# A hybrid decoder layer: sums of the features begun by item count instead of by the norm's factor, and another order of the first loads

## The chip, the core and the metric

The kernel runs on one core of a Trainium2 chip. A core has TensorE (matmuls; PE in the profile, with PEld for its weight loads), VectorE (DVE), ScalarE (ACT), GpSimd (POOL) and SyncE (SP), and 16 DMA engines that serve the queues of SP, ACT and POOL. The metric is the device time of one execution in microseconds; three runs of the kernel before took 2243.14, 2243.8 and 2244.31 us, the median is 2243.8.

## What is computed

One decoder layer on x of 256 tokens by 2048 features: a SwiGLU feed-forward, a token mixer (sliding-window attention beside an RWKV-7 recurrence), cross-attention into a memory of 256 tokens, a second SwiGLU feed-forward and a last norm. Only the first feed-forward and the last norm are touched:

```python
def rms_norm(x, g):
    y = xf * lax.rsqrt(jnp.mean(xf * xf, axis=-1, keepdims=True) + NORM_EPS)
    return (y * g.astype(jnp.float32)).astype(x.dtype)

def swiglu(h, w_gate, w_up, w_down):
    return (jax.nn.silu(h @ w_gate) * (h @ w_up)) @ w_down

x = x + 0.5 * swiglu(rms_norm(x, ffn1_norm[l]), ffn1_w_gate[l], ffn1_w_up[l], ffn1_w_down[l])
...
return rms_norm(x, final_norm)
```

The hidden width is 5632, so a gate or up matrix is 2048 x 5632 and 46 MB in float32. Everything is float32 in the reference.

## The kernel before

**Products.** Each float32 factor is split into a high part (rounded to the fp32r format) and the remainder. A product is three matmuls (lines 434 to 436): high by high, high by low, low by high. Weights come in units of two slabs of 128 rows by 512 columns. ScalarE makes the high part `hi` (line 357), VectorE the remainder `lo` (line 358), in rings of three buffers. Each use of a unit is an *item*: `next_item` hands out item i, and divides up to two units beyond it. In a plain product, an item is 12 matmuls (two slabs, two halves of the tokens, three matmuls).

**Seven products for eight.** In most of the feed-forward, gate and up are computed together, and for some items ("seven": 0, 2 and 4 of the eight pairs in a block of the first feed-forward) eight block products are replaced by seven, as in Strassen's and Winograd's schemes. This needs sums of weight slabs (`divide`, lines 386 to 389, split by `two_parts` into `thi` and `tlo`, lines 365 and 366) and sums and differences of the features (`combinations`, lines 466 to 485: sums on VectorE, a cast `chi` on ScalarE, the remainder `clo` on VectorE). A seven item is 21 matmuls, one of the others 24. The features' sums are made once for a feed-forward and used by all its pair products.

**The first feed-forward.** The norm's gain is applied to the features as they arrive (`Norm.features`: `xhi` in lines 653 and 655, `xlo` in line 656), the factor 1/rms only behind the products, since it is one number for each token. So the first block of gate (items 0 to 7) and of up (items 8 to 15) run as plain products while the sum of squares is still being made from x in its other layout (`tokens`, `squares`, line 667). `rstd` turns it into the factor `rs` (two small operations on VectorE, one power on POOL, lines 681 to 684). From item 16 on come the pairs, which need the sums of the features.

**Order of work.** A planner of the framework places the instructions on the engines from the order in which the program writes them. Background steps are Python generators; `bg.tick()` advances each group by one step, twice in a plain item. `combinations` is one of them: it does nothing until `ready()` holds, then takes three ticks for each of five pairs of features (0 to 4). The first pair product does not go on before they are all written (`bg.until(lambda: c["done"] ...)`). `tc.issue_after(at["lo"].ins)` puts a step behind the newest `lo` on VectorE; `at["hi"]` does so on ScalarE. In the kernel before, `ready()` is: the factor is written, and item 5 has begun.

**The first loads.** `cols` holds the gains, 16 columns of 128 partitions. `chunks(c, n)` loads n feature chunks of 128 features by 256 tokens, transposed, on SP's queue. `load(u, pieces)` loads weight units: in this stage a buffer holds four slabs (units u and u+1), of which there are four. Before, ScalarE's queue takes `cols` and the first slab; SP's takes features 0-1, slab 1, slabs 2-3, features 2-3, slabs 4-5, slabs 6-7, features 4-7 and so on.

Of the kernel before, what the change touches and what calls it, by code (L numbers as in the profile page):

```python
# [7 lines left out]
F32 = mybir.dt.float32  # L8
# [19 lines left out]
KU = 2  # L28
# [108 lines left out]
def decoder_layer(ctx: ExitStack, tc: tile.TileContext, a: dict, out: bass.AP):  # L137
# [102 lines left out]

    cols = cpool.tile([P, 163], F32, name="cols")
    cpool.tile([P, P], F32, name="pad")
    act.dma_start(cols[:, :KD], a["cols"][:, :KD])
    g_ffn1, g_mix, g_cross, g_mem, g_ffn2 = (cols[:, i * KD : (i + 1) * KD] for i in range(5))
    w0, a0, k_k, k_a, r_k, ln_w, ln_b = (cols[:, 80 + i * 8 : 88 + i * 8] for i in range(7))
    mu = cols[:, 136:163]
# [48 lines left out]
    def load(u, pieces=None):  # L295

        if u >= len(units) or u in raws:
            return
        w, k, c0, n = units[u]
        wide = at["pool"] is not None and (u < ends[0] or u >= ends[1] + LOADED)  # L300
        m = 2 if wide else 1
        if wide:
            raw = at["pool"].tile([P, m * KU, n], F32, tag="raw2", name="raw2", bufs=4)
        else:
            raw = wp.tile([P, KU, n], F32, tag="raw", name="raw", bufs=4)
        for i in range(m):
            raws[u + i] = raw[:, i * KU : (i + 1) * KU, :]
        if u in first_unused:
            second = u + 1 in first_unused
            pieces = [(slice(1, 2), nc.sync)] + [(slice(2 + second, 4), nc.sync)]  # L310
            if not second:
                pieces = ((slice(1, 4), nc.sync),)
        elif u + 1 in first_unused and wide:
            pieces = ((slice(0, 2), nc.sync), (slice(3, 4), nc.sync))
        for i, queue in pieces or ((slice(0, m * KU), nc.sync),):
            rows = slice((k + i.start) * P, (k + i.stop) * P)
            queue.dma_start(raw[:, i], w[rows, c0 : c0 + n].rearrange("(a p) n -> p a n", p=P))

    def load_sums(i):

# [367 lines left out]
    def feed_forward(sp, x, norm: Norm, wg, wu, wd, done, begin_last=lambda: None, last=False):  # L688
        if last:
            for tag, shape, dt, bufs in (  # L690
                ("hhi", [P, 16, T], F32R, 1), ("hlo", [P, 16, T], F32R, 1),
                ("hb", [P, 2, 512], F32, 2), ("thia", [P, KU, 512], F32R, 1),
                ("tloa", [P, KU, 512], F32R, 1), ("thib", [P, KU, 512], F32R, 1),
                ("tlob", [P, KU, 512], F32R, 1),
            ):
                sp.tile(shape, dt, tag=tag, name=tag, bufs=bufs)
        begun = at["item"]
        c = combinations(
            sp, norm.x, SEVEN_2 if last else SEVEN, "c", lambda: norm.r is not None and at["item"] > begun + 4
        )  # L700
        c["next"] = []
        for gi, (j0, nj) in enumerate(GROUPS):
            h = Act(
                [sp.tile([P, 16, T], F32R, tag="hhi", name="hhi")],
                [sp.tile([P, 16, T], F32R, tag="hlo", name="hlo")], 16,
            )
            ch = combinations(sp, h, SEVEN_DOWN[nj < 4], "d", early=False, n=12)

            def transposed(hb, c):
                for q in range(2):  # L710
                    split(h, c + 2 * q, 2, feat(hb, [2 * q * P, (2 * q + 1) * P]))
                    yield

            for j in range(j0, j0 + nj):
                if j > 0:
                    hb = gate_and_up(sp, norm.x, c, norm.r, wg)

                    c["next"].append(transposed(hb, 4 * (j - j0)))
                    continue
                pg = product(norm.x, wg)  # L720
                hb = sp.tile([P, 2, 512], F32, tag="hb", name="hb", bufs=2)
                if last:
                    for t in range(2):
                        act.activation(hb[:, t, :], pg[t][:], AF.Silu, scale=norm.r[t])
                pu = product(norm.x, wu, bank=acc if last else mm)
                bg.until(lambda: norm.r is not None)
                for t in range(2):
                    if not last:
                        act.activation(hb[:, t, :], pg[t][:], AF.Silu, scale=norm.r[t])
                    dve.scalar_tensor_tensor(  # L730
                        hb[:, t, :], pu[t][:], norm.r[t], hb[:, t, :], ALU.mult, ALU.mult
                    )
                c["next"].append(transposed(hb, 0))
            end = gi == len(GROUPS) - 1
            bg.spawn("feat", c["next"].pop())
            if end:
                begin_last()

            def col(t, n):
                return x[:, t, n * 512 : (n + 1) * 512]  # L740

            for n in (0, 2):
                if last and end and n:

                    whole = [(t, slice(0, 512)) for t in range(2)]
                    parts_ = [(t, slice(c, c + 256)) for t in range(2) for c in (0, 256)]
                    pieces = {2: whole, 3: parts_}
                    for m in (n, n + 1):
                        pd = product(h, wd, skew=m == 3)
                        for t, cs in pieces[m]:  # L750
                            dve.scalar_tensor_tensor(
                                col(t, m)[:, cs], pd[t][:, cs], 0.5, col(t, m)[:, cs],
                                ALU.mult, ALU.add,
                            )
                            done(m, t, cs)
                    continue
                down(sp, h, ch, wd, [[col(t, n + i) for i in range(2)] for t in range(2)])
                if end:
                    done(n)
                    done(n + 1)  # L760
# [17 lines left out]
    with tc.tile_pool(name="f1", bufs=1, reuse_waits="tile") as sp:  # L778
        aligned(sp)
        at["pool"] = sp  # L780
        x = sp.tile([P, 2, D], F32, name="x")

        def col(n):
            return x[:, :, n * 512 : (n + 1) * 512]

        n1 = Norm(g_ffn1)
        turned = f32(sp.tile([P, KD, T], F32R, tag="hlo", name="hlo")[:])

        def chunks(c, n):
            nc.sync.dma_start(turned[:, c : c + n], a["x_t"][:, c : c + n])  # L790

        chunks(0, 2)
        load(0, ((slice(0, 1), act), (slice(1, 2), nc.sync), (slice(2, 4), nc.sync)))
        act.copy(junk_t[:, :P], ones[:])
        chunks(2, 2)
        load(2, ((slice(0, 2), nc.sync), (slice(2, 4), nc.sync)))
        chunks(4, 4)
        load(4)
        chunks(8, 4)
        load(6)  # L800
        chunks(12, 4)

        def tokens(n):
            while at["item"] < 7 + n:
                yield
            with tc.issue_after(at["hi"].ins):
                act.dma_start(col(n), blk(W["x"], n))
            while at["item"] < 10 + n:
                yield
            n1.last = at["hi"]  # L810
            yield from n1.squares(n, col(n))

        for n in range(4):
            bg.spawn("stage", tokens(n))
        for n in range(4):
            bg.spawn("feat", n1.features(n, None, turned[:, 4 * n : 4 * n + 4], n == 0))
        bg.spawn("const", late_vectors())
        hold = {}

        def done1(n):  # L820
            if n == 0:
                hold["n"] = Norm(g_mix)
            pool.dma_start(blk(x1d, n), col(n))
            bg.spawn("feat", hold["n"].block(n, col(n)))

        feed_forward(sp, x, n1, W["ffn1_w_gate"], W["ffn1_w_up"], W["ffn1_w_down"], done1)
        n2 = hold["n"]
        bg.drain()
        at["pool"] = None
# [765 lines left out]
    with tc.tile_pool(name="f2", bufs=1, reuse_waits="tile") as sp:  # L1595
# [49 lines left out]
        )  # L1645
        bg.drain()
        for t in range(2):
            r = rstd(ss[:, t : t + 1, :])[0]
            for n in range(4):
                cb = slice(n * 512, (n + 1) * 512)  # L1650
                xs = x[:, t, cb]
                if n == 3:
                    dve.scalar_tensor_tensor(xs, xs, r, fin(n), ALU.mult, ALU.mult)
                elif n == 1:
                    dve.tensor_scalar(xs, xs, r, None, ALU.mult)
                else:
                    act.activation(xs, xs, AF.Copy, scale=r)
            for cb, queue in ((slice(0, 1024), nc.sync), (slice(1024, 1536), act),
                              (slice(1536, 2048), nc.sync)):
                queue.dma_start(out[0, t * P : (t + 1) * P, cb], x[:, t, cb])  # L1660
# [43 lines left out]
```

## Time and profile before

| | before |
|---|---|
| median of three runs | 2243.8 us |
| profiled execution, its own time | 2244.93 us |
| its span, first to last instruction | 2243.1 us |
| granted TensorE clock, mean | 0.997 |
| PE busy | 2224.4 us |
| DVE busy | 1824.4 us |
| ACT busy | 1247.8 us |
| DMA, mean over the span | 208 GB/s |

A row of the timeline reads: start in us, duration in us, engine, line, operation, output and inputs, shapes, and in brackets the idle time of the engine just before, with what ended it. A row of the list of waits reads: who waited for whom, total us, times, longest. A row of a table of stretches reads: from and to, length, busy time of PE, PEld, DVE, ACT and POOL with the number of instructions that begin there, then the granted TensorE clock (1.00 is full), the DMA share and GB/s. A row of the groups reads: line, engine, operation, tiles, shapes, count, busy us, mean ns, idle time before and what ended it. A matmul's recorded end is modelled and runs into the next one's start, so the pace is read from starts.

### The profile page before, as it was taken

To read this page: it belongs to the slowest core of one execution; us is meant where nothing else is said; L and a number is where in the kernel's file an instruction comes from. 1 tells how busy PE (TensorE), PEld (TensorE's weight loads), DVE (VectorE), ACT (ScalarE), POOL (GpSimd) and SP (SyncE) were. 2 spreads that over 40 slices of the span, in tenths; PEclk is the share of its full clock that TensorE was granted. 3 is DMA by queue.
4 is the path that set the end of the run, shared out by engine and by line. 5 is a ranking of instruction groups with operands and counts; after the bars stand their busy time and mean duration, and the time that the engine had idled before them with its cause. 6 is when DMAs were issued, how large, how long until landed. Compare 5 with 4: busy or idle time off the path is not lost.

```text
span 2243.1 us, 28143 instructions
## 1 busy us (share of the span) xinstructions
PE 2224.4 (99%) x10520; PEld 1825.1 (81%) x10520; DVE 1824.4 (81%) x2367; ACT 1247.8 (56%) x1625; POOL 121.3 (5%) x181
## 2 busy tenths in 40 slices
PE   9999999999999999999999999999999999999998
PEld 7788888888888877788888888888888888888877
DVE  6998988998989476977657666547999999999997
ACT  6455555554556468534444546556665465555654
POOL 0000000000000001210321030001000000000000
PEclk9999999999999999999999999999999999999999
DMA  8465565565556544676668678557565566556564
GB/s 302 167 208 188 207 206 188 197 208 195 193 195 207 177 144 143 191 232 209 215 209 270 203 261 283 188 167 272 198 239 204 194 237 214 202 204 223 197 225 150
DMA packets 231256, 466.02 MB, mean 208 GB/s; under 512 B 15472, under 2 KB 17616, under 8 KB 231120
## 3 DMA queue, kind: packets, MB, share of 16 engines
q1 hardware_dynamic: 221808, 437.82, 57.4%
q0 software_dynamic: 7648, 23.52, 3.4%
q10 hardware_dynamic: 1664, 2.89, 0.4%
q8 instruction: 82, 1.34, 0.2%
q14 instruction: 54, 0.44, 0.1%
HBM read 440.49 MB, written 23.59 MB: 207 GB/s over the span
## 4 chain that ended last, share of the span: by engine, by line
PE 93%; DVE 3%; DMA 2%; issue 1%; ACT 0%; SPq 0%; POOLq 0%; POOL 0%; DVEq 0%
PE acc L434 19%; PE acc L435 19%; PE acc L436 19%; PE mm L435 8%; PE mm L436 8%; PE mm L434 8%; PE tr L622 2%; PE tr L435 2%; PE tr L434 2%; PE tr L436 2%; PE mm L1344 1%; DVE lo L358 1%; DMA raw<-in_ffn_w_up_dram 1%; PE tr L1280 1%; PE mm L907 0%
## 5 line engine op out<-in xcount | busy, mean ns | idle before, releaser
L357 ACT CAST hi<-raw 128x1024 fp32r<-128x1024 f32 (+1 forms) x770 | 756.0, 992 | 702.4 <-PE acc L436 502.2
L358 DVE TENSOR_TENSOR lo<-raw,hi 128x1024 fp32r<-128x1024 f32 (+1 forms) x770 | 882.2, 1149 | 304.7 <-ACT hi L357 302.8
L434 PE MATMUL acc<-hi,xhi 128*128 128x512 f32 (+1 forms) x1134 | 448.8, 396 | 2.7 <-ACT xhi L655 1.3
L435 PE MATMUL acc<-lo,xhi 128*128 128x512 f32 (+1 forms) x1134 | 441.6, 389 | 3.8 <-DVE lo L358 3.8
L436 PE MATMUL acc<-hi,xlo 128*128 128x512 f32 (+1 forms) x1134 | 441.1, 389 | 0.0
L434 PEld LDWEIGHTS acc<-hi,xhi 128*128 128x128 f32 x1134 | 213.5, 188 | 50.0 <-issue 4.0
L435 PEld LDWEIGHTS acc<-lo,xhi 128*128 128x128 f32 x1134 | 213.7, 188 | 47.6 <-DVE lo L358 5.4
L436 PEld LDWEIGHTS acc<-hi,xlo 128*128 128x128 f32 x1134 | 213.5, 188 | 44.4 <-DVE xlo L656 0.6
L365 ACT CAST thi<-raw 128x1024 fp32r<-128x1024 f32 x192 | 199.7, 1051 | 69.2 <-DVE raw L388 48.4
L366 DVE TENSOR_TENSOR tlo<-raw,thi 128x1024 fp32r<-128x1024 f32 x192 | 232.4, 1219 | 1.1 <-ACT thi L365 0.4
L434 PE MATMUL mm<-hi,xhi 128*128 128x512 f32 x402 | 157.9, 393 | 0.0
L436 PE MATMUL mm<-hi,xlo 128*128 128x512 f32 x402 | 156.8, 390 | 0.0
L435 PE MATMUL mm<-lo,xhi 128*128 128x512 f32 x402 | 156.7, 390 | 0.0
L436 PE MATMUL acc<-hi,hlo 128*128 128x512 f32 x372 | 145.5, 391 | 0.0
L435 PE MATMUL acc<-lo,hhi 128*128 128x512 f32 x372 | 145.4, 391 | 0.0
L434 PE MATMUL acc<-hi,hhi 128*128 128x512 f32 x372 | 144.9, 390 | 0.0
L434 PEld LDWEIGHTS mm<-hi,xhi 128*128 128x128 f32 x402 | 75.5, 188 | 15.7 <-ACT hi L357 0.5
L436 PEld LDWEIGHTS mm<-hi,xlo 128*128 128x128 f32 x402 | 75.4, 188 | 15.8
L435 PEld LDWEIGHTS mm<-lo,xhi 128*128 128x128 f32 x402 | 75.5, 188 | 15.5
L434 PEld LDWEIGHTS acc<-hi,hhi 128*128 128x128 f32 x372 | 69.8, 188 | 14.3
L435 PEld LDWEIGHTS acc<-lo,hhi 128*128 128x128 f32 x372 | 69.9, 188 | 14.2
L436 PEld LDWEIGHTS acc<-hi,hlo 128*128 128x128 f32 x372 | 69.9, 188 | 14.0
(392 smaller groups left out, 3571.4 us busy)
## 6 DMA issues: line engine op xcount, KB each, us to landing
raw<-in_ffn_w_down_dram SPq DMA_DIRECT2D x88, 1024.0 KB, 5.2
raw<-in_ffn_w_gate_dram SPq DMA_DIRECT2D x84, 1024.0 KB, 5.1
raw<-in_ffn_w_up_dram SPq DMA_DIRECT2D x78, 1024.0 KB, 6.2
raw<-in_w_in_dram SPq DMA_DIRECT2D x136, 512.0 KB, 3.5
raw<-in_w_out_dram SPq DMA_DIRECT2D x32, 512.0 KB, 4.8
raw<-sums SPq DMA_DIRECT2D x20, 512.0 KB, 6.3
raw<-in_w_proj_attn_dram SPq DMA_DIRECT2D x16, 512.0 KB, 3.7
raw<-in_w_proj_rwkv_dram SPq DMA_DIRECT2D x16, 512.0 KB, 5.9
```

Source lines behind the costliest of these rows:

```text
L357: at["hi"] = act.copy(hi[:, s], raw[:, s])
L358: at["lo"] = dve.tensor_tensor(lo[:, s], raw[:, s], f32(hi[:, s]), ALU.subtract)
L365: act.copy(hi[:], v[:])
L366: dve.tensor_tensor(lo[:], v[:], f32(hi[:]), ALU.subtract)
L434: pe.matmul(o, xh, hi, start=first, stop=False, **how)
L435: pe.matmul(o, xh, lo, start=False, stop=False, **how)
L436: pe.matmul(o, xl, hi, start=False, stop=last, **how)
L622: pe.transpose(b[:, o : o + P], tok[:, t, col : col + P], ident[:])
L1280: pe.matmul(b[e][:, o : o + P], x1[r, j, cs_], x2[r, j, cs_], start=True, stop=True)
L1344: pe.matmul(vb[:, (o + k) * P : (o + k + 1) * P][:, r], lhs(k, e), rhs[:, k, r], start=first and k + e == 0, stop=True, **ek,)
```

## The change

Three parts. In the first feed-forward the sums of the features begin once item 8 has begun, whether or not the factor is written; the second keeps its condition (factor written and item 5 begun). The first transfers are put in another order: the gains go to SP's queue, both slabs of the first unit to ScalarE's, features 2-3 stand ahead of slabs 2-3, which the new `load_rest` loads. In the last norm the helper's three operations are written out.

```diff
-    act.dma_start(cols[:, :KD], a["cols"][:, :KD])
+    nc.sync.dma_start(cols[:, :KD], a["cols"][:, :KD])
...
+    def load_rest(u, c):
+
+        w, k, c0, n = units[u]
+        rows = slice((k + c) * P, (k + 2 * KU) * P)
+        nc.sync.dma_start(
+            raws[u + 1], w[rows, c0 : c0 + n].rearrange("(a p) n -> p a n", p=P)
+        )
...
         c = combinations(
-            sp, norm.x, SEVEN_2 if last else SEVEN, "c", lambda: norm.r is not None and at["item"] > begun + 4
+            sp, norm.x, SEVEN_2 if last else SEVEN, "c",
+            lambda: at["item"] > begun + (4 if last else 7) and not (last and norm.r is None),
         )
...
+        load(0, [(slice(c, c + 1), act) for c in range(2)])
+        act.copy(junk_t[:, :P], ones[:])
         chunks(0, 2)
-        load(0, ((slice(0, 1), act), (slice(1, 2), nc.sync), (slice(2, 4), nc.sync)))
-        act.copy(junk_t[:, :P], ones[:])
         chunks(2, 2)
+        load_rest(0, 2)
         load(2, ((slice(0, 2), nc.sync), (slice(2, 4), nc.sync)))
...
-            r = rstd(ss[:, t : t + 1, :])[0]
+            m, r = (stat.tile([P, 1], F32, tag=e, name=e) for e in ("ms", "rs"))
+            dve.tensor_reduce(m[:], ss[:, t : t + 1, :], AX.X, ALU.add)
+            dve.tensor_scalar(m[:], m[:], 1.0 / D, EPS, ALU.mult, ALU.add)
+            pool.tensor_tensor(r[:], m[:], nhalf[:, :1], ALU.pow)
```

## The prediction, made before the changed kernel was run

> **What bounds the kernel now.** I read the page's totals first, then what TensorE waited for, then the stretches around those waits.
>
> ```profile
> span 2243.1 us, 28143 instructions
> PE 2224.4 (99%) x10520; PEld 1825.1 (81%) x10520; DVE 1824.4 (81%) x2367; ACT 1247.8 (56%) x1625; POOL 121.3 (5%) x181
> ...
> PE acc L435 <- DVE lo L358: 3.8, 1, 3.8
> PE acc L434 <- ACT xhi L655: 1.3, 2, 0.9
> ```
>
> TensorE is busy in 99% of the span, so an edit can win only where TensorE stands still or runs slowly. The list of waits (total, times, longest) has one large entry: a single wait of 3.8 us for a weight remainder `lo` from VectorE. The next, 1.3 us, lies in the start-up. The timeline of TensorE shows the place: the crossing from the plain products of the first feed-forward (items 0 to 15 of the weight plan) to the seven-product pairs (from item 16).
>
> ```profile
> 52.51 0.39 PE L434 MATMUL mm<-hi,xhi 128*128 128x512 f32 x1
> ...
> 59.35 0.93 PE L434 MATMUL mm<-hi,xhi 128*128 128x512 f32 x2
> 64.06 0.80 PE L435 MATMUL acc<-lo,xhi 128*128 128x512 f32 x1 [3.79 <-DVE lo L358]
> 64.65 0.63 PE L436 MATMUL acc<-hi,xlo 128*128 128x512 f32 x1
> 65.08 0.63 PE L434 MATMUL acc<-hi,xhi 128*128 128x512 f32 x1
> ...
> 70.17 0.39 PE L436 MATMUL mm<-hi,clo 128*128 128x512 f32 x1
> ...
> 71.56 0.39 PE L434 MATMUL tr<-thi,chi 128*128 128x512 f32 x1
> ```
>
> Between 52.51 and 71.56 us the timeline has 46 matmuls. After the wait they start 0.43 us apart (64.65, 65.08) instead of 0.23, until 70.17. The granted clock (the number behind POOL in the next rows) says why: it halves while TensorE waits and returns near 70 us.
>
> ```profile
> 63.00:63.50 0.50, 0.00 (x0) 0.00 (x0) 0.50 (x1) 0.00 (x0) 0.00 (x0) 0.78 0.00 0
> 63.50:64.00 0.50, 0.00 (x0) 0.00 (x0) 0.50 (x2) 0.00 (x0) 0.00 (x0) 0.50 0.00 0
> ...
> 70.00:71.00 1.00, 1.00 (x5) 0.80 (x5) 1.00 (x2) 0.63 (x1) 0.00 (x0) 0.95 1.02 387
> ```
>
> What the crossing costs needs the undisturbed pace. The second feed-forward makes the same crossing from the same code, at 1580.40, with its sums finished 7.5 us ahead (VectorE's last `clo`, 1572.24 + 0.69):
>
> ```profile
> 1572.24 0.69 DVE L485 TENSOR_TENSOR clo<-raw,chi 128x512 fp32r<-128x512 f32 x1
> ...
> 1580.40 0.39 PE L434 MATMUL tr<-thi,chi 128*128 128x512 f32 x1
> ...
> 1591.96 0.39 PE L434 MATMUL mm<-hi,xhi 128*128 128x512 f32 x1
> ...
> 1573.00:1583.00 10.00, 10.00 (x46) 8.28 (x45) 10.00 (x13) 5.28 (x6) 0.00 (x0) 1.00 0.67 226
> ```
>
> From 1580.40 to 1591.96 there are 51 steps: 11.56 / 51 = 0.2267 us each, without a pause. So 46 matmuls should take 10.4 us, and the first crossing takes 71.56 - 52.51 = 19.05: **8.6 us are lost**. Of these 3.8 are the wait, about 2.8 the halved clock (14 steps from 64.06 to 70.17: 6.11 - 14 x 0.2267 = 2.9), the rest small gaps.
>
> Why VectorE is late stands in its rows before and after 46 us:
>
> ```profile
> 28.00:46.00 18.00, 18.00 (x81) 14.89 (x80) 7.70 (x9) 12.68 (x24) 0.43 (x1) 1.00 0.94 338
> ...
> 46.00:72.00 26.00, 21.83 (x78) 16.05 (x77) 26.00 (x47) 14.21 (x19) 1.50 (x3) 0.87 0.39 125
> ...
> L466 DVE TENSOR_TENSOR raw<-xhi,xlo 128x512 f32<-128x512 f32 x5 | 3.2, 683 | 0.0
> L472 DVE TENSOR_TENSOR raw<-raw 128x128 f32<-128x128 f32 x3 | 0.9, 284 | 0.0
> L478 DVE TENSOR_TENSOR raw<-raw 128x256 f32<-128x256 f32 x2 | 0.8, 418 | 0.0
> L485 DVE TENSOR_TENSOR clo<-raw,chi 128x512 fp32r<-128x512 f32 (+1 forms) x5 | 2.8, 577 | 0.0
> ```
>
> The third number after the length is VectorE: 7.70 us busy of 18 up to 46 us, then 26.00 of 26. The sums of x sit in the full stretch, because they wait for the factor `rs`, which POOL begins at 45.57:
>
> ```profile
> 45.57 0.70 POOL L684 TENSOR_TENSOR rs<-ms,nhalf 128x2 f32<-128x2 f32 x1 [44.16 <-DVE ms L682]
> ```
>
> **The change part by part.** First, the sums. Five groups, 24 VectorE instructions: L466 x5, L472 to L475 x3 each (all four lines are like the L472 row), L478 x2, L485 x5. Their busy times add up to 3.2 + 4 x 0.9 + 0.8 + 2.8 = 10.4 us; each next one starts some 0.08 us before its forerunner's recorded end, so they take 10.4 - 24 x 0.08 = 8.5 us of the engine. The new condition is item 8 instead of the factor. A group takes three ticks, there are two ticks per item, so 15 ticks spread over items 7 to 14. Item 8 begins at 30.75 (row below) and each item is 12 matmuls, 2.72 us, so this is about 28 to 50 us. By then the features are done (their steps end with item 6 in the code). VectorE has 18 - 7.70 = 10.3 us free from 28 to 46 us; 8.5 us fit, with little over.
>
> Does that early work delay something? Each stage is queued behind the newest `lo`, so the next `lo` can wait for one stage, at most about 1.4 us (L466 and four short ones: 0.6 + 4 x 0.2).
>
> ```profile
> 30.75 0.39 PE L434 MATMUL mm<-hi,xhi 128*128 128x512 f32 x1
> ...
> 32.03 1.23 DVE L358 TENSOR_TENSOR lo<-raw,hi 128x1024 fp32r<-128x1024 f32 x1 [1.50 <-ACT hi L357]
> ```
>
> This `lo` belongs to item 10, is done at 33.26 and is first used at 30.75 + 2 x 2.72 = 36.19: 2.9 us of slack. So the early sums cost nothing while that holds; without it, each microsecond beyond is one of TensorE. Behind the removed sums VectorE runs 8.5 us ahead after 46 us. What is late next is the weight work of the second seven-product item, item 18:
>
> ```profile
> 69.41 1.22 DVE L366 TENSOR_TENSOR tlo<-raw,thi 128x1024 fp32r<-128x1024 f32 x1
> ```
>
> Its first `tlo` moves from 69.41 to 60.9 and is done at 62.1, while item 17 ends at 52.51 + 45 x 0.2267 = 62.7. It just fits. The gain is bounded by 8.6 (all lost time back); from below by 6.6, if the wait and the slow clock go and the small gaps stay; a gain of nothing has the row against it that TensorE waited for VectorE alone. I take 8.3, nearer the upper end, because the second feed-forward's row shows 10.00 of 10.00 with VectorE also full.
>
> ScalarE gets the five casts of the sums earlier as well, into a stretch where it is busy 12.68 of 18:
>
> ```profile
> 47.27 1.27 ACT L729 ACTIVATE hb<-acc,rs 128x512 f32<-128x512 f32 x2
> ...
> L365 ACT CAST thi<-raw 128x1024 fp32r<-128x1024 f32 x2 | 2.1, 1051 | 1.0 <-DVE raw L388 1.0
> L482 ACT CAST chi<-raw 128x512 fp32r<-128x512 f32 (+1 forms) x5 | 2.6, 531 | 3.7 <-DVE raw L475 2.9 <-DVE raw L478 0.7
> ```
>
> They are 2.6 us at most. Behind them come the SiLU at 47.27, a cast `hi` and a cast `thi` (1.05 each) and `tlo` (1.22). If the SiLU slipped by all 2.6, the first `tlo` would be done at 49.9 + 1.3 + 2.1 + 1.2 = 54.5, 2.0 us after item 16 begins at 52.51; that end is in the range. With 5.3 us free I take no slip.
>
> Second, the start. These rows carry it:
>
> ```profile
> 0.81 0.41 ACTq L243 DMA_DIRECT2D cols<-in_cols_dram  x1
> 1.26 0.45 ACTq L317 DMA_DIRECT2D raw<-in_ffn_w_gate_dram  x1
> ...
> 6.23 0.73 PE L434 MATMUL acc<-hi,xhi 128*128 128x512 f32 x2 [0.96 <-ACT hi L357]
> ...
> 7.30 1.14 ACT L357 CAST hi<-raw 128x512 fp32r<-128x512 f32 x2 [0.60 <-DMA raw<-in_ffn_w_gate_dram]
> ...
> 13.40 1.71 ACT L655 ACTIVATE xhi<-hlo,cols 128x256 fp32r<-128x256 f32 x4 [0.19 <-DMA hlo<-in_x_t_dram]
> 13.96 0.50 PE L434 MATMUL acc<-hi,xhi 128*128 128x512 f32 x1 [0.90 <-ACT xhi L655]
> ```
>
> The first weight slab becomes the first transfer of ScalarE's queue (0.81 instead of 1.26), the second slab moves there from SP, and the gains go to the head of SP's queue, past features 0-1. Features 2-3 pass the 512 KB of weight rows 2-3. On SP six issues stand before features 4-7 both ways; POOL's queue is untouched. Item 0 needed the second transfer of ScalarE's queue and now needs the second of SP's, so it begins near 6 us as before. Weight rows 2-3 land behind 256 KB more, 0.9 us at 284 GB/s (below): cast from 8.2 instead of 7.30, item 1 from 8.8, done at 11.6. But item 2 waits for features 4-7, which land at 13.40, and ahead of them on the two queues lie the same bytes: 2 MB of weights, 1 MB of features with themselves, 8 KB of gains. So the start is worth nothing past 13.96 unless the bytes flow faster. They might: with both queues at work from 4 to 6 us the rate is 381 GB/s, then 284 with SP alone:
>
> ```profile
> 4.00:6.00 2.00, 1.27 (x6) 0.98 (x5) 1.41 (x4) 0.44 (x1) 0.00 (x0) 1.00 1.03 381
> 6.00:8.00 2.00, 1.77 (x7) 1.17 (x8) 1.34 (x3) 1.40 (x4) 0.00 (x0) 1.00 0.99 284
> ```
>
> 256 KB more on the second queue, beside as much on the first, at 381 instead of 284 GB/s: 524 KB take 1.38 instead of 1.85 us, 0.5 us sooner. The lower bound is a loss of 0.4, one issue slot of SP. I take a gain of 0.2. The Trainium skill (DMA: Bandwidth & Descriptors, Issuing engines are not separate DMA queues) speaks against a faster flow: transfers of all issuing engines end on the same 16 DMA engines, and a second issuer saves only issue time. By that rule the 0.2 is 0, and the sum 0.2 us worse.
>
> Third, the last norm's factor: the helper's three operations are written out, with the same operands. Nothing is added or removed: 0.
>
> Sum: 8.3 + 0.2 = 8.5. The profiled execution took 2244.93 us (1.8 us beside its span), so it would take 2236.4. It lies 1.1 above the median of 2243.8; from the median the forecast is **2235.3**.
>
> **The rivals.** (a) Another engine takes the wait's place: ScalarE's SiLU slips, or VectorE's free 10.3 us don't hold all of the sums. For it: only 1.8 us of VectorE's are over. Then up to the 2.0 us worked out above stay: 2237.3. (b) The start pays with the clock. Items 0 and 1 end sooner, while item 2 stays at 13.96, so scattered waits become one. In the rows above the clock fell some 3 us after the last matmul (60.28 to about 63.3). If item 1 ended before 11, the clock would halve until some 20 us, for the 2.9 us it cost at 64.06: 2238.2. Against it: weight rows 2-3 landed at 7.30 and can't land sooner behind more bytes, so item 1 ends at 7.30 + 0.6 (cast) + 2.7 = 10.6 at the earliest, more likely at the 11.6 above. The Trainium skill (TensorE: Matmul & The Clock Gate, What's actually happening) puts the idle window at about 3.4 us and free-running; by it a gap of 2.4 us leaves the clock alone. (c) It does not do what it says, because the planned order keeps the sums late: 2243.8. Against it: the code emits them before items 15 and 16. (d) The other side: the casts of the sums stand on ScalarE behind squares that wait for x from memory, VectorE then waits for a cast ahead of the next `lo`, and TensorE stops. It decides once a block of x is more than the 2.9 us of slack late. Two such stops at 3.8 + 2.8 each cost 13.2, less 8.5 gained: 2248.5. Against it: the squares (128x512, eight of them) waited 0.1 us in all.
>
> ```profile
> L667 ACT ACTIVATE junk<-x 128x512 bf16<-128x512 f32 x8 | 5.0, 630 | 0.1
> ```
>
> **How the numbers follow.** Forecast 0.72, (a) 0.13, (b) 0.07, (c) 0.05, (d) 0.03. About 0.2% (4.5 us) can be told from no change here. The forecast, (a) and (b) lie more than that below: 0.92, less 0.02 for a larger slip in (a), so faster 0.90, same 0.07, slower 0.03. The range runs from 2234.0 (8.6 and 0.5 gained, and 0.7 of scatter: the three runs reach from 2243.14 to 2244.31) to 2238.4, which takes in (a) and (b).
>
> **What would show it.** TensorE's list should lose the 3.8 us entry; its clock stay at 1.00 from 52 to 72 us; `clo` be finished before 50; item 18's first `tr` matmul come near 63 instead of 71.56. The first plain matmul should stay within 0.6 us of 6.23, and item 2's within 0.5 us of 13.96. It would be wrong if a wait for `tlo` or `thi` stands at 52 to 63 us, if `lo` comes late between 30 and 50, or if the clock falls before 20.

## The result, and the profile after

The changed kernel takes **2237.95 us** (median of 10 runs, 2237.37 to 2238.39) against 2243.47 us for the kernel before in the same comparison (10 runs, 2242.46 to 2244.50): ratio 0.9975, 95% interval 0.9965 to 0.9984, so 5.5 us faster. The forecast was 2235.3, its range 2234.0 to 2238.4. The sign and the mechanism came as forecast; the measured gain is 5.5 us where 8.5 were forecast.

The page's totals after, and the first entries of TensorE's list of waits:

```profile
span 2235.6 us, 28143 instructions
PE 2220.6 (99%) x10520; PEld 1823.4 (82%) x10520; DVE 1823.0 (82%) x2367; ACT 1247.3 (56%) x1625; POOL 121.3 (5%) x181
```

```profile
PE acc L443 <- DVE lo L366: 1.1, 2, 0.9
...
PE acc L442 <- DVE xhi L661: 0.6, 1, 0.6
PE tr L442 <- ACT thi L373: 0.5, 1, 0.5
```

The work is the same (28143 instructions); the span is 7.5 us shorter. The profiled execution itself took 2237.5 us. The single wait of 3.8 us is gone: what is left for `lo` (1.1 us in two pieces) lies in the start. (Lines are 8 higher than before: `lo` is now L366, the matmuls L442 to L444, `thi` and `tlo` L373 and L374, the sums L474 to L493.) A new entry stands there, 0.5 us for `thi`. The timeline of TensorE shows where:

```profile
30.64 0.39 PE L442 MATMUL mm<-hi,xhi 128*128 128x512 f32 x1
...
52.17 0.39 PE L444 MATMUL mm<-hi,xlo 128*128 128x512 f32 x1
53.01 0.72 PE L442 MATMUL tr<-thi,chi 128*128 128x512 f32 x2 [0.46 <-ACT thi L373]
...
64.13 0.62 PE L442 MATMUL tr<-thi,chi 128*128 128x512 f32 x2
```

52.17 is the last matmul of item 15, so item 16 was due one step later, at 52.40. That agrees with 96 steps of 0.2267 from item 8's first (30.64 + 21.76), and so the crossing can be read in every run of this case as the time from item 8 + 21.76 us to item 18's first `tr`. Here it is 64.13 - 52.40 = **11.73 us**, against 19.05 before and 10.43 for 46 undisturbed steps. Of the 8.6 us lost, 7.3 came back; 1.3 are still lost. Together with the start (item 8 at 30.64 instead of 30.75) that is 7.4 of the 7.5 us between the two spans. The third part of the change is worth nothing, as forecast: from the last norm's last `x<-acc` to its `x<-x,rs` it takes 2.34 us (2227.44 to 2229.78) and took 2.35 (2234.96 to 2237.31).

One caution for the runs below: the planner does not always put the same matmuls ahead of item 18's first `tr`. Here, and in the kernel before, one matmul of item 18 stands ahead of it, so that the crossing has 46 steps; where it has 45 or 48, this is said, and what is lost is counted against that number of steps.

What is still lost shows on VectorE and ScalarE. First the two stretches of before, now after:

```profile
28.00:46.00 18.00, 18.00 (x81) 14.92 (x80) 14.02 (x24) 12.97 (x25) 0.00 (x0) 1.00 0.95 339
46.00:72.00 26.00, 25.49 (x110) 20.17 (x110) 25.21 (x37) 17.14 (x21) 2.23 (x3) 1.00 0.49 158
```

VectorE did 14.02 us in the first stretch instead of 7.70. Of the 24 instructions in it 6 are `lo` and 18 belong to the sums, so 18 of the 24 instructions of the sums were moved ahead, some 6.7 us and not 8.5 (6.3 by the difference, which lacks the 0.3 us of `ms` that stood in this stretch before). The clock stays at 1.00. VectorE's timeline behind 46 us names what was not moved, the fifth group of sums (L474, L480 to L483, L493):

```profile
46.56 1.23 DVE L366 TENSOR_TENSOR lo<-raw,hi 128x1024 fp32r<-128x1024 f32 x1 [0.84 <-ACT hi L365]
47.70 0.15 DVE L689 TENSOR_REDUCE ms<-ss 128x2 f32<-128x8 f32 x1
47.77 0.68 DVE L474 TENSOR_TENSOR raw<-xhi,xlo 128x512 f32<-128x512 f32 x1
...
51.06 1.22 DVE L366 TENSOR_TENSOR lo<-raw,hi 128x1024 fp32r<-128x1024 f32 x1
52.19 0.68 DVE L493 TENSOR_TENSOR clo<-raw,chi 128x512 fp32r<-128x512 f32 x1
52.79 0.68 DVE L397 TENSOR_TENSOR raw<-raw,raw 128x512 f32<-128x512 f32 x1
53.40 1.22 DVE L374 TENSOR_TENSOR tlo<-raw,thi 128x1024 fp32r<-128x1024 f32 x1
```

The engine was free for 0.84 us just before 46.56: it was not short of time there, but the fifth group was queued behind that `lo`. The first `tlo` ends at 54.6; the prediction's bad case said 54.5. On ScalarE the SiLU slid from 47.27 to 49.72, since the last square before it began at 46.43 instead of 44.29, and `thi` slid with it:

```profile
49.72 1.27 ACT L738 ACTIVATE hb<-acc,rs 128x512 f32<-128x512 f32 x2 [0.21 <-POOL rs L692]
...
51.91 1.05 ACT L373 CAST thi<-raw 128x1024 fp32r<-128x1024 f32 x1
```

The start moved little. The first plain matmul, and item 2's first, which waits for features 4-7:

```profile
5.91 0.70 PE L442 MATMUL acc<-hi,xhi 128*128 128x512 f32 x2 [0.64 <-DVE xhi L661]
...
13.86 0.50 PE L442 MATMUL acc<-hi,xhi 128*128 128x512 f32 x1 [0.33 <-ACT xhi L663]
```

### The profile page after: what moved, and what is told of

The parts are those of the page before. It is cut to its first block, busy times and chain, and to the rows that moved or that the text cites. A ratio compares the mean times of both kernels' runs of the same rounds, so it can differ in the third digit from the quotient of the medians.

```text
span 2235.6 us, 28143 instructions
## 1 busy us (share of the span) xinstructions
PE 2220.6 (99%) x10520; PEld 1823.4 (82%) x10520; DVE 1823.0 (82%) x2367; ACT 1247.3 (56%) x1625; POOL 121.3 (5%) x181
## 4 chain that ended last, share of the span: by engine, by line
PE 93%; DVE 3%; DMA 2%; issue 1%; ACT 1%; POOL 0%; SPq 0%; POOLq 0%; ACTq 0%; DVEq 0%
PE acc L442 19%; PE acc L443 18%; PE acc L444 18%; PE mm L444 8%; PE mm L443 8%; PE mm L442 8%; PE tr L443 2%; PE tr L630 2%; PE tr L442 2%; PE tr L444 2%; DVE lo L366 1%; PE mm L1354 1%; PE tr L1290 1%; DMA raw<-in_ffn_w_up_dram 0%; PE mm L917 0%
## 5 line engine op out<-in xcount | busy, mean ns | idle before, releaser
L366 DVE TENSOR_TENSOR lo<-raw,hi 128x1024 fp32r<-128x1024 f32 (+1 forms) x770 | 881.0, 1147 | 295.2 <-ACT hi L365 293.5
L442 PE MATMUL acc<-hi,xhi 128*128 128x512 f32 (+1 forms) x1134 | 448.3, 396 | 1.4 <-DVE xhi L661 0.6
L444 PE MATMUL acc<-hi,xlo 128*128 128x512 f32 (+1 forms) x1134 | 440.0, 388 | 0.0
L442 PEld LDWEIGHTS acc<-hi,xhi 128*128 128x128 f32 x1134 | 213.2, 188 | 48.5 <-issue 4.9
L444 PEld LDWEIGHTS acc<-hi,xlo 128*128 128x128 f32 x1134 | 212.9, 188 | 44.1 <-DVE xlo L664 0.5
L373 ACT CAST thi<-raw 128x1024 fp32r<-128x1024 f32 x192 | 199.7, 1052 | 65.3 <-DVE raw L396 44.8
L374 DVE TENSOR_TENSOR tlo<-raw,thi 128x1024 fp32r<-128x1024 f32 x192 | 232.0, 1217 | 1.3 <-ACT thi L373 0.6
L442 PE MATMUL mm<-hi,xhi 128*128 128x512 f32 x402 | 157.9, 393 | 0.1
L444 PE MATMUL mm<-hi,xlo 128*128 128x512 f32 x402 | 156.7, 390 | 0.0
L444 PE MATMUL acc<-hi,hlo 128*128 128x512 f32 x372 | 145.5, 391 | 0.0
L442 PE MATMUL acc<-hi,hhi 128*128 128x512 f32 x372 | 144.9, 390 | 0.0
L442 PEld LDWEIGHTS mm<-hi,xhi 128*128 128x128 f32 x402 | 75.5, 188 | 15.8 <-ACT hi L365 0.5
L444 PEld LDWEIGHTS mm<-hi,xlo 128*128 128x128 f32 x402 | 75.4, 188 | 15.8
L442 PEld LDWEIGHTS acc<-hi,hhi 128*128 128x128 f32 x372 | 69.9, 188 | 14.3
L444 PEld LDWEIGHTS acc<-hi,hlo 128*128 128x128 f32 x372 | 69.9, 188 | 14.0
```

The costliest lines, as they stand in the source:

```text
L366: at["lo"] = dve.tensor_tensor(lo[:, s], raw[:, s], f32(hi[:, s]), ALU.subtract)
L373: act.copy(hi[:], v[:])
L374: dve.tensor_tensor(lo[:], v[:], f32(hi[:]), ALU.subtract)
L442: pe.matmul(o, xh, hi, start=first, stop=False, **how)
L444: pe.matmul(o, xl, hi, start=False, stop=last, **how)
```

## The experiments

Times are medians. "Before" is the kernel before, run on the same chip in the same comparison.

### Each half alone, and the kernel before once more

The sums alone (the kernel before, with the new condition only):

```diff
-            sp, norm.x, SEVEN_2 if last else SEVEN, "c", lambda: norm.r is not None and at["item"] > begun + 4
+            sp, norm.x, SEVEN_2 if last else SEVEN, "c",
+            lambda: at["item"] > begun + (4 if last else 7) and not (last and norm.r is None),
```

> The early sums alone, with the loads in the old order. If the whole gain comes from the crossing into the pairs, the median is 5.0 to 5.7 us under the kernel before, item 16 to the first tr of item 18 takes 11.7 us as in the changed kernel, and item 2 starts at 13.96. If the loads carry some of it, the gain is under 4.5 us.

The loads alone (the kernel after, with this edit taken back, so that it also keeps the third part):

> The new order of loads alone, with the sums waiting for the factor. By the same bytes ahead of features 4-7 the time is within 0.5 us of the kernel before, item 2 starts at 13.8 to 13.9, and the 3.8 us wait with the halved clock is there again. If the loads carried 1 us or more of the gain, item 2 would start before 13.

The kernel before, without an edit, for a second profile:

> The kernel before once more, for its trace: the profiled execution took 2244.93, its median is 2243.47. If the halved clock varies from run to run, the stretch at 0.43 us a matmul is shorter or begins elsewhere in a faster run, and the crossing (52.51 to 71.56, 19.05 us) changes by as much as the time. If the scatter lies elsewhere, the crossing takes 19.05 us within 0.1 again.

Measured: the sums alone 2236.96 us against 2243.82, ratio 0.9969 (0.9957 to 0.9981); the loads alone 2244.65, ratio 1.0004 (0.9995 to 1.0013). The sums carry the whole gain; the loads carry none that can be told. The kernel before took 2243.53 us in its second profile, and it differs from the first in two places that make up the 1.40 us between the two executions: item 8 begins at 29.93 instead of 30.75 (0.82), and the crossing takes 18.45 instead of 19.05 (0.60). In the loads alone, which keeps the late sums, the crossing takes 17.83. All three have the same stop (3.8 us); what differs is the clock. Its rows, in stretches of 1 us, for the kernel before in its second profile:

```profile
61.00:62.00 1.00, 0.00 (x0) 0.00 (x0) 1.00 (x5) 0.00 (x0) 0.00 (x0) 0.59 0.00 0
62.00:63.00 1.00, 0.00 (x0) 0.00 (x0) 1.00 (x2) 0.00 (x0) 0.00 (x0) 0.50 0.00 0
...
67.00:68.00 1.00, 1.00 (x4) 0.81 (x3) 1.00 (x2) 0.97 (x2) 0.00 (x0) 0.50 0.97 377
68.00:69.00 1.00, 1.00 (x6) 0.77 (x6) 1.00 (x3) 0.83 (x3) 0.00 (x0) 1.00 1.01 360
```

and for the loads alone:

```profile
64.00:65.00 1.00, 0.93 (x4) 0.79 (x5) 1.00 (x3) 0.62 (x1) 0.00 (x0) 1.00 0.00 0
65.00:66.00 1.00, 1.00 (x5) 0.76 (x4) 1.00 (x3) 0.00 (x0) 0.00 (x0) 0.60 0.89 88
...
68.00:69.00 1.00, 1.00 (x5) 0.81 (x4) 1.00 (x2) 1.00 (x2) 0.00 (x0) 0.70 1.00 373
```

A mean of 0.59 between 1.00 and 0.50 means a fall 0.18 us into the stretch: the clock is halved from 61.18 to 68.00 in the first (6.8 us, of which 2.1 lie in the stop itself) and from 65.20 to 68.60 in the second (3.4 us, all of it behind the stop). So the halved clock cost the matmuls half of 4.7 = 2.4 us there, half of 3.4 = 1.7 here, and 2.9 in the profile on which the prediction rests. The same stop has three prices.

### Beginning the sums earlier

The change, with the condition met two items sooner; then the same with the old loads:

```diff
-            lambda: at["item"] > begun + (4 if last else 7) and not (last and norm.r is None),
+            lambda: at["item"] > begun + (4 if last else 5) and not (last and norm.r is None),
```

> The changed kernel with the sums begun two items sooner (item 6 instead of 8). The 1.5 us that the crossing still loses came from the fifth group of sums and the casts that lie in the squares' stretch. If so, the SiLU goes back to 47.3 to 48.5, the 0.5 us wait for thi is gone, item 16 to the first tr of item 18 takes 10.4 us, and the median is 1.0 to 1.5 us under the changed kernel (2236.5 to 2237.0). If the loss has another cause, or the features' remainders on VectorE push back, it is the same as the changed kernel within 0.3 us, or slower.

> Early sums from item 6, loads in the old order. If the new order of loads costs time, as 29.5 us (sums alone) against 30.6 us (changed kernel) for the first matmul of item 8 suggests, this is 0.5 to 1.0 us under the version from item 6 with the new loads (2236.23): 2235.2 to 2235.7, item 8 begins between 29.5 and 30.0. If the start only scatters from run to run, whatever the order, it is 2236.2 within 0.4, and item 8 begins anywhere from 29.5 to 30.8.

Measured: 2236.23 against 2243.82, ratio 0.997 (0.9959 to 0.9981); with the old loads 2235.89 against 2243.63, ratio 0.9963 (0.9951 to 0.9976). The rows of the first, TensorE at both ends of the crossing, VectorE's fifth group, and the first stretch:

```profile
52.22 0.39 PE L442 MATMUL tr<-thi,chi 128*128 128x512 f32 x1
...
62.64 0.39 PE L442 MATMUL tr<-thi,chi 128*128 128x512 f32 x1
```

```profile
46.49 0.68 DVE L493 TENSOR_TENSOR clo<-raw,chi 128x512 fp32r<-128x512 f32 x1
...
51.00 1.23 DVE L374 TENSOR_TENSOR tlo<-raw,thi 128x1024 fp32r<-128x1024 f32 x1 [0.73 <-ACT thi L373]
```

```profile
28.00:46.00 18.00, 18.00 (x81) 14.92 (x80) 16.22 (x28) 13.67 (x26) 0.00 (x0) 1.00 0.96 334
```

The crossing takes 62.64 - 52.22 = 10.42 us; it has 45 steps here, 10.20 us undisturbed, so 0.2 us are lost instead of 1.3. With the old loads it takes 10.47, also for 45. The wait is gone. All sums but the last `clo` (46.49) now stand ahead of 46 us, and VectorE still had gaps of 0.66 and 0.89 us between them. So the free time was enough, and what failed was the assumption that the new condition brings all five groups ahead of 46 us. (That 16.22 - 7.70 gives 8.5, the prediction's figure, is chance: four of the 24 instructions ran ahead of 28, and a slab sum of the weights lies inside.) The intervals of both ratios overlap with the change's own, so it is the traces that show this, not the medians.

### What keeps the fifth group late: the SiLU, or its place in VectorE's queue

The change, with the SiLU of a seven-product item held behind its last `thi`:

```diff
-                        act.activation(hb[:, t, :], pg[t][:], AF.Silu, scale=norm.r[t])
+                        with tc.issue_after(at["thi"].ins):
+                            act.activation(hb[:, t, :], pg[t][:], AF.Silu, scale=norm.r[t])
```

> The changed kernel (sums from item 8, new loads) with the SiLU of the first product held behind the last cast thi of item 16. If the SiLU's slip from 47.27 to 49.72 is what makes the first thi late, the 0.5 us wait for thi goes and item 16 to the first tr of item 18 takes 10.6 to 11.0 us instead of 11.7: 0.8 us under the changed kernel. If VectorE's fifth group of sums sets it, thi comes at 51.1 at the earliest, and the stretch stays at 11.4 us or more. If the SiLU then frees its banks too late, a new wait appears in item 16.

Measured: 2238.68 against 2243.63, ratio 0.9977 (0.9968 to 0.9987). ScalarE's part goes (the first `tr` is on time, at 52.15), and nothing is won. VectorE, then TensorE:

```profile
52.55 0.69 DVE L397 TENSOR_TENSOR raw<-raw,raw 128x512 f32<-128x512 f32 x1
53.15 1.22 DVE L374 TENSOR_TENSOR tlo<-raw,thi 128x1024 fp32r<-128x1024 f32 x1
```

```profile
52.15 0.62 PE L442 MATMUL tr<-thi,chi 128*128 128x512 f32 x2
...
56.45 0.50 PE L442 MATMUL acc<-thi,xhi 128*128 128x512 f32 x1 [0.83 <-ACT hb L739]
```

`tlo` still starts at 53.15, since VectorE goes from one instruction to the next without a gap, and the late SiLU makes a wait of its own. The crossing is 64.44 - 52.15 = 12.29 us for 46 steps. The SiLU's slip is not what has to be mended.

The change, with the steps of the sums queued behind the `lo` and `hi` of two units earlier (`at["lo2"]`, as it stood two divisions ago) in place of the newest:

```diff
+        for e in ("hi", "lo"):
+            at[e + "2"], at[e + "1"] = at.get(e + "1"), at.get(e)
...
-                with tc.issue_after(at["lo"].ins):
+                with tc.issue_after(at["lo" + pin].ins):
...
+            pin="" if last else "2",
```

> The change, with the steps of the sums queued behind the lo and hi of two units earlier in place of the newest. If it is the place behind the newest lo that leaves VectorE's fifth group until after 46 us, its first sum (the line with raw<-xhi,xlo) now stands ahead of item 15's two last lo, the slab sums of item 16 begin earlier, the first tlo starts at or before 52.9 instead of 53.40, the 46 matmuls of the crossing take 10.4 to 11.2 us instead of 11.73, and the time is 0.5 to 1.3 us under the change's. If it is not the place but the number of ticks, the last clo stays behind 51 us, the crossing stays above 11.4 and the time within 0.3 us of the change's.

Measured: 2237.04 against 2243.39, ratio 0.997 (0.9958 to 0.9981), 0.57 us under the whole change on the same chip (2237.61), with runs that overlap (2236.51 to 2238.08 and 2236.38 to 2238.57); the reading rests on the trace. VectorE:

```profile
41.53 0.69 DVE L476 TENSOR_TENSOR raw<-xhi,xlo 128x512 f32<-128x512 f32 x1
...
49.06 0.69 DVE L495 TENSOR_TENSOR clo<-raw,chi 128x512 fp32r<-128x512 f32 x1 [0.47 <-ACT chi L492]
...
52.58 1.22 DVE L376 TENSOR_TENSOR tlo<-raw,thi 128x1024 fp32r<-128x1024 f32 x1 [1.09 <-ACT thi L375]
```

The fifth group begins at 41.53 instead of 47.77, its `clo` is at 49.06 instead of 52.19, and the crossing takes 63.52 - 52.70 = 10.82 us for 45 steps, 0.6 more than undisturbed: 0.7 of the 1.3 us come back with the same condition and the same number of ticks. VectorE now waits 1.09 us for `thi`; that the rest is ScalarE's is not shown by an experiment. Place and start act alike: the first sum begins at 26.76 here and at 26.28 with the earlier start, instead of 30.34, and either brings the fifth group ahead of the crossing.

### The order of the loads

The whole change and the sums alone once more, on one chip:

> The kernel with the whole change once more, on one chip with the next one. If the new order of the loads costs something, it is 0.3 to 1.2 us slower than the sums alone with the old loads; if it costs nothing, the medians lie within 0.3 us and their intervals overlap for the most part. The forecast's term for it, 0.2 us gained, would put it 0.2 below.

> The new condition of the sums with the old order of the loads. If the loads are the dearer half of the change, item 8 begins 0.3 to 1.2 us sooner here than in the whole change and the time is less by as much; if they are worth nothing, both kernels are within 0.3 us of each other.

Measured: 2237.61 (ratio 0.9972, 0.9960 to 0.9983) and 2237.35 (ratio 0.9970, 0.9958 to 0.9981) against 2243.39. 0.26 us apart, with runs from 2236.38 to 2238.57 and 2235.97 to 2238.01: not told apart. Their crossings are the same, 11.76 and 11.75 us, and item 8 begins at 30.83 and 30.66. Over the profiles of this case item 8 begins at 29.51 to 30.75 with the old order (7 profiles, mean 30.20) and at 30.39 to 30.94 with the new one (6 profiles, mean 30.67). That speaks for a loss of some 0.5 us, but the spread of the old order is 1.2 us and no timed pair resolves it. Most of the spread lies in when features 4-7 come: their cast `xhi` begins between 12.14 and 13.40 with the old order and between 12.57 and 13.36 with the new one.

The old-loads kernel with the earlier sums, and features 4-7 put ahead of the weight rows that pass them:

```diff
-        load(2, ((slice(0, 2), nc.sync), (slice(2, 4), nc.sync)))
-        chunks(4, 4)
+        chunks(4, 2)
+        load(2, ((slice(0, 2), nc.sync),))
+        chunks(6, 2)
+        load_rest(2, 2)
```

> The version before it, with features 4-5 ahead of weight rows 4-5 and features 6-7 ahead of rows 6-7, in place of 512 + 512 KB of weights and then 512 KB of features. If item 2 waits for the bytes ahead of its features, it starts at 12.4 to 12.9 instead of 13.4 to 13.9, item 8 begins 0.8 to 1.3 us sooner and the median is lower by as much (2234.0 to 2234.8). If the pace of the first DMAs or the casts set it, nothing moves by more than 0.4 us.

Measured: **2235.35** against 2243.63, ratio 0.9962 (0.9948 to 0.9975); the same kernel without the edit took 2235.89. The last matmul of item 1, the first of item 2, and item 8:

```profile
12.12 0.39 PE L444 MATMUL acc<-hi,xlo 128*128 128x512 f32 x1
12.35 0.62 PE L442 MATMUL acc<-hi,xhi 128*128 128x512 f32 x2
...
28.70 0.39 PE L442 MATMUL mm<-hi,xhi 128*128 128x512 f32 x1
```

Item 2 follows item 1 without a pause, at 12.35 instead of 13.80. The cast of features 4-5 begins at 10.70 instead of 12.45, ahead of that of all 13 other profiles. Item 8 begins 1.44 us sooner (28.70 instead of 30.14), the crossing stays at 10.47. So the bytes ahead of features 4-7 set when these come, and the change leaves these bytes as they were. But not all of the 1.44 us is theirs: in the profile without the edit the matmuls ran at half pace until about 10.3 (see the end), which held up items 0 and 1. The timed gain, 0.5 us, is within the scatter of five runs each; the spans differ by 1.2 us, and later waits grew (for `ga`, from 0.4 to 0.7 us). It is the fastest kernel of this case, 8.3 us below the kernel before.

### The price of the halved clock by itself

The kernel before, with small matmuls of ones into a spare accumulator ahead of the stop, 7 and then 18 of them (each is two records in the trace):

```diff
+            if "kept" not in at:
+                at["kept"] = acc()
+                with tc.issue_after(at["mm"].ins):
+                    for _ in range(18):
+                        pe.matmul(at["kept"][:, :P], ones[:], ones[:], start=True, stop=True)
```

> The kernel before, sums late, with seven matmuls of a tile of ones by itself put on TensorE ahead of the wait for lo in item 17; they write a bank that nobody reads. If the pause of 3.8 us lets the clock fall and the fall costs 1.6 to 2.9 us, the clock stays at 1.00 from 60 to 72 us, the steps behind the wait are 0.227 us, and the kernel is 1.5 to 2.9 us faster than before with the same VectorE work. If the slow steps have another cause (operands late, the memory), they stay at 0.43 us and the time is the same or up to 3 us more.

> The kernel before, with 18 small matmuls of ones into a spare accumulator (some 3.9 us, never read) ahead of the wait for the sums of x, so that TensorE is hardly idle there. Nothing of the result is changed. If the halved clock is a price of its own, the clock stays at 1.00 from 52 to 72 us in every run, and the kernel gains 1.5 to 2.9 us on the kernel before, with runs no more than 1.5 us apart. If the slow steps are not from the clock but from operands that come late, the steps behind the wait stay near 0.43 us and the time within 0.5 us of the kernel before. If the small matmuls last longer than the wait, the gain is less by what they overrun, up to 0.5 us.

Measured: with 7, 2243.16 against 2243.63, ratio 0.9996 (0.9987 to 1.0005), with runs from 2240.95 to 2244.55; with 18, **2240.50** against 2243.39, ratio 0.9986 (0.9977 to 0.9995), with runs from 2239.29 to 2242.36. The seven lasted only 1.72 us and left 2.50 us of the stop; the profiled execution kept its clock all the same (and lost 5.8 us in the crossing, as with 18), but the median shows no gain. The eighteen fill it:

```profile
58.66 4.18 PE L549 MATMUL acc<-ones 128*128 128x128 f32 x36
62.59 0.71 PE L434 MATMUL mm<-hi,xhi 128*128 128x512 f32 x2
63.36 0.51 PE L435 MATMUL acc<-lo,xhi 128*128 128x512 f32 x1
63.71 0.39 PE L436 MATMUL acc<-hi,xlo 128*128 128x512 f32 x1
63.94 0.40 PE L434 MATMUL acc<-hi,xhi 128*128 128x512 f32 x1
```

```profile
62.00:63.00 1.00, 1.00 (x10) 0.87 (x8) 1.00 (x2) 0.00 (x0) 0.00 (x0) 1.00 0.00 0
63.00:64.00 1.00, 0.94 (x5) 0.55 (x4) 1.00 (x3) 0.46 (x1) 0.00 (x0) 1.00 0.00 0
64.00:65.00 1.00, 1.00 (x6) 0.82 (x5) 1.00 (x2) 0.16 (x1) 0.00 (x0) 1.00 0.57 45
```

The steps behind the stop are 0.23 us (63.71, 63.94), though the sums are as late as before: the matmul that waited for `lo` starts 33.31 us after item 8 here (63.36 - 30.05), and 33.31, 33.31 and 33.33 us after it in the two profiles of before and in the loads alone. The operands were there, and the slow steps of before were the clock's. The crossing takes 68.49 - 51.81 = 16.68 us. Three matmuls of item 18 stand ahead of its `tr` here, so it has 48 steps, 10.88 us undisturbed, and 5.8 us are lost; with the halved clock 8.6, 8.0 and 7.4 were lost. So by the traces the clock costs 2.8, 2.2 and 1.6 us, within 0.2 of the 2.9, 2.4 and 1.7 above; by the medians 2.9 (1.1 to 5.2 by the interval). The runs lie 3.1 us apart, not the 1.5 that was expected, with a mean granted clock of 0.999 in all eleven, so the clock isn't the only source of scatter.

## Why the prediction was right, and where it was not

**Right.** The wait was for the sums, and it went with them: the sums alone gain 6.9 and 6.0 us in two comparisons, the loads nothing. The clock is a price of its own, as the split into 3.8 and about 2.8 had it: with TensorE kept at work the clock stayed up and 2.9 us came back while the sums were still late. The early sums cost nothing where they went: TensorE is busy 18.00 of 18 us from 28 to 46. VectorE had the room for all the sums, as the earlier start showed. Item 2 stays at 13.86 (13.96 before, forecast within 0.5), the first plain matmul at 5.91 (6.23, within 0.6).

**Wrong: "15 ticks spread over items 7 to 14".** The step counted ticks and free time, but not that each stage is queued behind the newest `lo` and the last ones behind item 15's. So 18 of 24 instructions were moved ahead, 6.7 us and not 8.5; `clo` ended at 52.9, not before 50; item 18's first `tr` came at 64.13, not near 63; its first `tlo` at 63.72, not 60.9. One of the signs that the prediction named against itself came too: TensorE waited for `thi` at 53.01, if only 0.46 us. Starting two items earlier mends it (0.2 us lost instead of 1.3), loosening the place does by half (0.6). The term of 8.3 came out at 7.3 in the trace.

**Wrong: "With 5.3 us free I take no slip".** The SiLU slid by 2.45 us, because ScalarE's free time lay elsewhere than in front of it, and `tlo` came out as in the bad case. But this slip alone is not what costs: with the SiLU moved away, `tlo` was as late. Of rival (a), which had 0.13 and 2237.3 us, it is therefore VectorE's half that came true; not because the free 10.3 us were too few, as (a) had it, but because the instructions stood behind others. That the time (2237.95) landed nearer to (a) than to the forecast is luck for the most part: the crossing lost only 1.0 us more than forecast, and the rest of the 2.65 us has other reasons (below).

**Wrong: the 0.2 us for the start.** No timed pair shows a gain; the first pair of profiles has 0.1 for it (30.64 against 30.75), all of them together speak for a loss up to 0.5, which is the lower bound's size (0.4). The faster flow did not come: from 4 to 6 us the rate was 289 GB/s instead of 381, from 6 to 8 us 348 instead of 284, and from 5 to 20 us the core moved 380 GB/s before and 382 after.

```profile
5.00:20.00 15.00, 12.71 (x51) 8.88 (x50) 11.03 (x18) 10.71 (x18) 0.00 (x0) 1.00 1.03 380
```

```profile
5.00:20.00 15.00, 12.94 (x52) 9.02 (x51) 11.66 (x20) 10.19 (x17) 0.00 (x0) 1.00 1.03 382
```

By the rule of the Trainium skill that the prediction weighed against it (DMA: Bandwidth & Descriptors, Issuing engines are not separate DMA queues) the term was 0; these rows agree.

**Wrong: the step from the profiled execution to the median.** 2236.4 was forecast for an execution like the profiled one, and 1.1 us were taken off because that lay 1.1 above the median. That step would be right if the surplus lay where the change does nothing. By the second profile of before, 1.40 us shorter, 0.82 of it lies ahead of item 8, which the change leaves, but 0.60 in the crossing, where the change takes the loss away whatever its size. An execution with less to lose there gains less, so by this pair some 0.5 of the 1.1 came off twice; two profiles don't settle the figure. In all, the 2.65 us between forecast and median are 1.0 missing from the sums and 0.1 from the start (2236.4 against the profiled 2237.5), the 1.1 of this step, and 0.45 by which the profiled execution after lies below its own median.

**The other rivals.** (b) came in part, and by another condition than it gave. In three of the six profiles with the new loads the clock fell before 20 us, as the prediction had it among its signs of being wrong, but while items 0 and 1 ran: in the one that begins the sums two items earlier it is halved from 7.7 to 11.1 (last section). The price was small. Item 8 begins 17.31 to 17.36 us after the cast of features 4-7 in the seven profiles with a pause ahead of item 2, and 17.47 to 17.93 us after it in these three, so 0.1 to 0.6 us were lost there, not 2.9. (c) fell with the first profile after, and so did (d): no wait for `lo` stands between 30 and 50 us.

## What to carry to other kernels

Work that is moved ahead has to be placed, not only fitted in: an engine's free time says that the work can be done there, and what it is queued behind says when it will be; ask which is the last of the moved instructions and what stands in front of it. A stop of the matmul engine costs its length and a price for the clock that differs from one execution to the next, so a loss read from one profile is one sample; take a second profile before its terms are subtracted from a median. And where a start is bound by transfers, count the bytes ahead of the operand that is waited for last: an order that leaves them alone leaves the time alone.

## What the runs showed of the hardware

The clock changes in steps of one length. It was halved for 6.82 us (63.28 to 70.10 in the first profile of before, 61.18 to 68.00 in the second), for 3.40 (65.20 to 68.60 in the loads alone) and, in the start of the kernel that begins the sums two items earlier, for 3.40 again:

```profile
7.00:8.00 1.00, 0.61 (x2) 0.55 (x3) 1.00 (x3) 0.81 (x2) 0.00 (x0) 0.85 1.04 403
8.00:9.00 1.00, 1.00 (x3) 0.76 (x3) 0.73 (x2) 0.52 (x2) 0.00 (x0) 0.50 1.04 399
...
11.00:12.00 1.00, 1.00 (x5) 0.80 (x5) 0.99 (x1) 0.42 (x1) 0.00 (x0) 0.95 1.02 389
```

And it is not tied to the stop: it fell 3.0 us after TensorE's last matmul in the first profile of before, 1.7 after it in the second, and in the loads alone 1.1 us after the matmuls had begun again. The Trainium skill (TensorE: Matmul & The Clock Gate, What's actually happening) gives a window of 3413 ns that runs freely, and these traces agree: 3.40 and 6.82 are one and two of these lengths. They show it over the whole kernel too: in the six profiles with a fall in the first 70 us the clock falls once more after the kernel's last matmul, and the two falls lie 636, 637 or 651 times 3.4133 us apart, to within 0.01 us (for the kernel before 2237.57 - 63.28 = 2174.29, which is 637 times 3.4133). So the boundaries at which the clock can change are fixed within an execution and lie elsewhere in the next one. That is why the same stop cost 1.7, 2.4 and 2.9 us.

A window need not be idle for a fall. With the boundaries counted back from the last fall of each of the 14 profiles, a clock that stood at 1.00 fell behind every window in which TensorE was busy for 1.67 us or less (by the profile, which models the ends of matmuls), and behind none with 1.81 us or more; the line lies near half of the 3.41 us. In the second profile of before the window ahead of the fall held 1.67 us of matmuls; in the one with seven small matmuls the two windows of the stop held 2.51 and 1.81, and the clock stayed up. So gaps far shorter than the 2.4 us that rival (b) took to be harmless are enough: in the start shown above the window up to 7.69 has no gap over 1.0 us, but holds only 1.58 us of matmuls.

The record of the clock has a gap at the start. In four profiles (the second of before, the loads alone, the second of the sums alone, and the earlier start with the old loads) the first matmuls begin 0.43 us apart while the clock's row reads 1.00. The last of these slow steps begin at 9.81, 10.40, 9.25 and 10.00, and the boundaries counted back from the end lie at 9.97, 10.58, 9.55 and 10.28, each within that step. So the clock was halved there, and the record missed it.
